# RWKV's triangular-inverse joins dealt among projections, and softmax's 1/sum put on a diagonal in the transposes

## Chip, cores and metric

The kernel runs on one core of one Trainium2 chip. The metric is the device time of one execution in microseconds (us), the median over runs. The engines are PE (matrix multiply; its weight loads are PEld), DVE (vector), ACT (scalar), POOL (GpSimd) and SP (which issues most DMAs). They work side by side, each through its own instructions in program order, and wait for one another by semaphores.

## What is computed

Two blocks of a language model over 1024 tokens of width 1024, in float32. The first is attention, cross attention and an MLP. The second block, in which the change lies, projects its input, mixes tokens in three ways at once and projects back:

```python
h = _rmsnorm(x, g_pre) * (1.0 + scale[:, None]) + shift[:, None]
proj = h @ w_in
...
attn = _sliding_window_attention(aq, ak, av, sinks)      # 8 heads, window 128, softmax with a sink
rwkv = _rwkv7_mixer(h, rr, rk, rv, ...)                  # 4 heads, a recurrence over tokens
gla = _gla_mixer(h, gq, gkk, gv, ...) * jax.nn.silu(gg)  # 4 heads, gated linear attention
y = jnp.concatenate([attn, rwkv, gla], axis=-1) @ w_out
return x + gate[:, None] * _rmsnorm(y, g_post)
```

The sliding attention's core is a softmax of which one column, the sink, is dropped again, and RWKV's recurrence is one step per token:

```python
p = jax.nn.softmax(jnp.concatenate([s, sink], axis=-1), axis=-1)[..., :-1]
o = jnp.einsum('bnhgqk,bnkhd->bnqhgd', p.astype(v.dtype), vb)
...
sa = jnp.einsum('bhvk,bhk->bhv', S, -kk_t)
S = (S * w_t[:, :, None, :] + sa[..., None] * (kk_t * a_t)[:, :, None, :]
     + v_t[..., None] * k_t[:, :, None, :])
```

## The kernel before, in words

Tokens go in two chunks of 512. For each chunk the second block has a stage for RWKV and GLA (`g_rec`, L1730) and one for the sliding attention (`g_window`, L1617; `g_window0` for chunk 0, `g_tail`, L1639, for chunk 1). `block2` (L1290) runs them in the order: chunk 0's `g_rec`, chunk 0's window, chunk 1's `g_rec`, chunk 1's window (called the tail below), then `finish`, which ends the output projection and the final norm of chunk 1.

PE has two sorts of work in these stages. The projections (`g_proj_F`, then the output projection `g_wout2`/`g_wout2a`) are long rows of 512-column matmuls at L210, L211 and L212: three per slice of 128 input rows, since each float32 product is made of high and low parts. They need nothing from the mixers. The mixers' own matmuls are small and hang on one another through DVE, ACT and POOL. `weave` (L144) deals the first out among the second: a mixer is a Python generator that yields a number after each piece; a positive number is the piece's own cost in ns and is multiplied by a ratio, a negative one is taken in full as a wait to be covered, and `weave` lets that many ns of projection slices (648 ns a slice) be issued there. The scheduler behind the language then moves single instructions within what the data allow, so the order on an engine is told by the built program. These projection matmuls are called fill below.

In `g_rec`, `early` (L1926) does RWKV. For 32 units (8 sub-chunks of 64 tokens by 4 heads) it inverts a triangular 64x64 matrix. First `s1` (L1780, L1786) makes the matrices with four groups of transposes and matmuls; `s2a` and `s2a_` (L1808, L1818) are PE work that hangs only on ACT. DVE alone solves the 16x16 diagonal blocks: four transposes (L1945), 15 steps of multiply and add (L1955, L1958), then two transposes that give TD (L1969) and more that fill U (L1978) and TQ. Then come the joins, which build the rest by matmuls on 32-row pieces:

- join 1, L1986: 64 matmuls with TD, which DVE turns into Y (L1988);
- join 2, L1994 and L1997: 96 matmuls with U and Y, copied out by ACT (L1998) and DVE (L2000);
- join 3, L2006: 32 matmuls, copied by ACT;
- join 4, L2013: 32 matmuls, copied by ACT.

A plain float32 matmul leaves two records in the trace, so the counts there are doubled. After the joins come `s2b` (L1828), `s2c` (L1842) and the recurrence `s3` (L1864 to L1881), with ACT and DVE steps between, and GLA's chain (`_gla`), whose main matmuls are L2156.

`w_units` (L1646) does the sliding attention, in 8 units per chunk (4 blocks of 128 queries by 2 groups of 4 heads). A unit's `a()` makes scores (L1668, L1669), adds the bias (DVE L1671), takes maxima (L1672), exponentials with their sums (ACT L1679), the reciprocal of the sum with the sink (DVE L1682, L1683), and then scales the probabilities `p` by it: two heads on ACT (L1685), two on POOL (L1686). `tr()` transposes each 128x128 piece of `p` on PE with the identity (L1700) and copies it out of PSUM (ACT L1703); `pv()` multiplies by the values (L1710), and DVE gates the result (L1712). A unit has 8 transposes, but 4 in each of the first two of chunk 0, so there are 120.

Beside the tail's output projection, `g_final0` (L2328) ends chunk 0's final norm. It is a generator as well, and `g_wout2a` (L2309) calls its next step after every second slice (after each in the first column block). Its first steps make a sum over partitions (L226), its inverse root (DVE L219, POOL L220) and two broadcasts by PE (L234), of `rf` and of `rz`; the others load, scale, add (DVE L2344, L2346, POOL L2347) and store one row block each.

Of the kernel before, what the change touches and what calls it, by code (L numbers as in the profile page):

```python
# [12 lines left out]
F32 = mybir.dt.float32  # L13
# [157 lines left out]
class K:  # L171
# [1118 lines left out]
    def block2(s, wp, pre, out):  # L1290
        tc, nc = s.tc, s.nc
        with tc.tile_pool(name="b2", bufs=1, reuse_waits="tile") as b2, tc.tile_pool(name="wk3", bufs=2, reuse_waits="tile") as s.wk, tc.tile_pool(
            name="smC", bufs=4, reuse_waits="tile"
        ) as s.sm:
            s.vt = b2.tile([P, NB, 400], F32, name="vt")
            s.b2_consts(b2)
            with tc.tile_pool(name="lo", bufs=1, reuse_waits="tile") as s.lop:
                with tc.tile_pool(name="wt", bufs=1, reuse_waits="tile") as wt:
                    with tc.tile_pool(name="pp", bufs=2, reuse_waits="tile") as pp:
                        vt = s.vt_load(wt, wp)  # L1300

                        def beside(m):
                            if m == 1:
                                hi = s.tl(s.xp, [P, KT, CH], "act", F32R)
                                lo = s.lop.tile([P, KT, CH], F32R, tag="lo1", name="lo1")
                                s.slow = s.fin_steps(1, hi, lo, s.wk)
                            for _ in range(2 if m >= 2 else 0):
                                next(vt, None)
                            if m == 7:
                                for _ in vt:  # L1310
                                    pass

                        for _ in chain(s.g_p2a(pp, 0, pre, beside), s.g_vt()):
                            pass
                rest = s.g_p2b(1)
                weave(
                    s.g_rec(0), chain(s.g_p2b(0), s.take(rest, s.K0)),
                    0.45
                )
                with tc.tile_pool(name="pp", bufs=2, reuse_waits="tile") as pp:  # L1320
                    weave(
                        s.g_window0(), chain(s.g_p2a(pp, 1), s.take(rest, s.K1)),
                        0.9
                    )
                    while s.steps:
                        s.steps.pop(0)()
                tp = ExitStack()

                def tail():
                    yield from s.g_tail(tp.enter_context(tc.tile_pool(name="tp", bufs=1, reuse_waits="tile")))  # L1330

                main = chain(s.g_rec(1), tail())
                rest = chain(rest, s.g_wout2(b2), s.g_wout2a(s.g_final0(b2, out)))
                weave(main, rest, 0.45, False)
                with tp, tc.tile_pool(name="fp", bufs=1, reuse_waits="tile") as fp:
                    s.finish(fp, wp, out, rest)

# [308 lines left out]
    def w_units(s, wn, c, qst, kst, bias, sink, one):  # L1646
# [6 lines left out]
        def unit(b, g):  # L1653
# [7 lines left out]
            def a():  # L1661
                p = u["p"] = wn.tile([P, 4, 2 * P], F32, tag="wp", name=s.nm("wp"), bufs=3)
                t = s.sm.tile([P, 6, 4], F32, tag="wt", name=s.nm("wt"))
                for z in range(2):
                    ps = s.ps([P, 2, 2 * P])
                    for y in range(2):
                        q = qst[2 * z + y][g][:, (b % 4) * P : (b % 4 + 1) * P]
                        mm(ps[:, y, :w], q, kst[g][:, k0 : k0 + w], start=True, stop=False)  # L1668
                        mm(ps[:, y, :w], q, kst[2 + g][:, k0 : k0 + w], start=False, stop=True)  # L1669
                    pz = p[:, 2 * z : 2 * z + 2, :w]  # L1670
                    V.scalar_tensor_tensor(pz, ps[:, :, :w], 0.125, bs[:, 2 * z : 2 * z + 2, :], ALU.mult, ALU.add)  # L1671
                    V.tensor_reduce(t[:, 0, 2 * z : 2 * z + 2], pz, AX.X, ALU.max)  # L1672
                sk = sink[:, 4 * g : 4 * g + 4]
                V.tensor_tensor(t[:, 1, :], t[:, 0, :], sk, ALU.max)
                V.tensor_tensor(t[:, 2, :], sk, t[:, 1, :], ALU.subtract)
                V.tensor_scalar(t[:, 1, :], t[:, 1, :], -1.0, None, ALU.mult)
                nc.scalar.activation(t[:, 2, :], t[:, 2, :], AF.Exp)
                for h in range(4):
                    nc.scalar.activation(  # L1679
                        p[:, h, :w], p[:, h, :w], AF.Exp, bias=t[:, 1, h : h + 1], accum_out=t[:, 3, h : h + 1]  # L1680
                    )
                V.tensor_tensor(t[:, 3, :], t[:, 3, :], t[:, 2, :], ALU.add)  # L1682
                V.reciprocal(t[:, 4, :], t[:, 3, :])  # L1683
                for h in range(2):
                    nc.scalar.activation(p[:, h, :w], p[:, h, :w], AF.Copy, scale=t[:, 4, h : h + 1])  # L1685
                nc.gpsimd.tensor_tensor(  # L1686
                    p[:, 2:4, :w], p[:, 2:4, :w], t[:, 4, 2:4, None].to_broadcast([P, 2, w]), ALU.mult
                )

            def tr():  # L1690
# [6 lines left out]
                for z in range(nk):  # L1697
                    ps = s.ps()
                    for h in range(4):
                        nc.tensor.transpose(ps[:, h * P : (h + 1) * P], u["p"][:, h, z * P : (z + 1) * P], s.ident)  # L1700
                    t = one[:, 4 + st["n"] % 4, :]
                    st["n"] += 1
                    nc.scalar.activation(t, ps, AF.Copy)  # L1703
# [41 lines left out]
    def rwkv(s, rp, ra, c):  # L1745
# [180 lines left out]
        def early():  # L1926
# [56 lines left out]
            for k in range(32):  # L1983
                for z in range(2):
                    a = slice(32 * z, 32 * z + 32)
                    mm(ps[a, k, :], XU[a, k, 1, a], TD[a, k, :], start=True, stop=True)  # L1986

            V.scalar_tensor_tensor(  # L1988
                Y, ps[0:64], s.m16[0:64, 0:1], s.m16[0:64, None, 1:17].to_broadcast([64, 32, 16]), ALU.mult, ALU.add
            )  # L1990
            yield -2000
            ps, pq = s.ps([P, 32, 16]), s.ps([P, 32, 16])
            for k in range(32):
                mm(pq[0:32, k, :], U[0:32, k, 0:32], Y[0:32, k, :], start=True, stop=True)  # L1994
                for z in range(2):
                    a = slice(32 * z, 32 * z + 32)
                    mm(ps[32 * z : 32 * z + 16, k, :], Y[a, k, :], U[a, k, 32 * z + 16 : 32 * z + 32], start=True, stop=True)  # L1997
            act(TQ[0:32, :, 0:16], pq[0:32], AF.Copy)  # L1998
            for z in range(2):
                V.tensor_copy(U[32 * z : 32 * z + 16, :, 32 * z + 16 : 32 * z + 32], ps[32 * z : 32 * z + 16])  # L2000
            yield 2000
            for g in range(2):
                ps = s.ps([P, 16, 32])
                for i in range(16):
                    k = 16 * g + i
                    mm(ps[32:64, i, :], XU[0:32, k, 1, 32:64], TQ[0:32, k, :], start=True, stop=True)  # L2006
                act(TQ[32:64, 16 * g : 16 * g + 16, :], ps[32:64], AF.Copy)
                yield 1000
            for g in range(2):
                ps = s.ps([P, 16, 32])  # L2010
                for i in range(16):
                    k = 16 * g + i
                    mm(ps[0:32, i, :], TQ[32:64, k, :], U[32:64, k, 32:64], start=True, stop=True)  # L2013
                act(U[0:32, 16 * g : 16 * g + 16, 32:64], ps[0:32], AF.Copy)
                yield (3860, 1000)[c]

            s2b(0)
            yield (1190, 1744)[c]
# [309 lines left out]
    def g_final0(s, b2, out):  # L2328
# [1 line left out]
        nc = s.nc  # L2330
        V = nc.vector
        r = s.sm.tile([P, 4], F32, tag="rz", name=s.nm("rz"))
        yield
        s.rsq(r, s.sums(s.zacc), 1.0 / D, EPS)
        RF = s.rst
        s.bcast(RF, s.rf[:, 0:4])
        yield
        RZ = s.zacc
        s.bcast(RZ, r)
        for mt in range(KT):  # L2340
# [113 lines left out]
```

## Time and profile before

| | |
|---|---|
| median of 3 runs | 2352.42 us (lowest 2352.35) |
| profiled execution: its time, its span from first to last instruction | 2354.5, 2352.7 us |
| busy share of the span: PE, DVE, ACT, POOL | 96%, 53%, 44%, 29% |
| mean granted PE clock, share of 2.4 GHz | 0.968 |
| second block's stages, from the first `s1` to the end | 1728.4 to 2352.7 us |

PE's busy time is modelled from starts, so a PE that is always busy can still be slow: its clock is granted at 2.4 or 1.2 GHz, and the share of it is given for each stretch as PEclk. A stretch of the trace is read by three things: how long PE waited and for whom, at which clock it ran, and what stood in its queue.

### The profile page before, as it was taken

To read this page: it belongs to the slowest core of one execution; us is meant where nothing else is said; L and a number is where in the kernel's file an instruction comes from. 1 tells how busy PE (TensorE), PEld (TensorE's weight loads), DVE (VectorE), ACT (ScalarE), POOL (GpSimd) and SP (SyncE) were. 2 spreads that over 40 slices of the span, in tenths; PEclk is the share of its full clock that TensorE was granted. 3 is DMA by queue.
4 is the path that set the end of the run, shared out by engine and by line. 5 is a ranking of instruction groups with operands and counts; after the bars stand their busy time and mean duration, and the time that the engine had idled before them with its cause. 6 is when DMAs were issued, how large, how long until landed. Compare 5 with 4: busy or idle time off the path is not lost. (4 is left out here: it accounts for less than half of the span.)

```text
span 2352.7 us, 36021 instructions
## 1 busy us (share of the span) xinstructions
PE 2255.0 (96%) x13696; PEld 1908.1 (81%) x13696; DVE 1251.6 (53%) x2266; ACT 1035.5 (44%) x2198; POOL 689.2 (29%) x1035
## 2 busy tenths in 40 slices
PE   8999999999999999999999999999999998999886
PEld 7898999988898888888888888888787875777765
DVE  7665656676754555423423322346842667526574
ACT  6655656674643424411311312344533357333563
POOL 4101100000500003566666630036321443214443
PEclk9999999999999999999999999999998999969997
DMA  4010010123241211222222211143342333424452
GB/s 135 28 41 23 30 39 28 46 78 122 68 137 54 99 36 50 77 74 79 83 74 79 79 59 51 48 134 121 116 128 76 113 121 118 147 74 134 154 173 75
DMA packets 116541, 200.14 MB, mean 85 GB/s; under 512 B 14192, under 2 KB 33936, under 8 KB 115600
## 3 DMA queue, kind: packets, MB, share of 16 engines
q1 hardware_dynamic: 111600, 184.73, 24.4%
q0 software_dynamic: 4768, 13.11, 1.7%
q8 instruction: 107, 1.75, 0.3%
q14 instruction: 66, 0.54, 0.1%
HBM read 163.71 MB, written 34.08 MB: 84 GB/s over the span
## 5 line engine op out<-in xcount | busy, mean ns | idle before, releaser
L210 PE MATMUL ps<-act,wh 128*128 128x512 f32 x1664 | 667.2, 404 | 8.8 <-ACT wh L202 5.4
L212 PE MATMUL ps<-act,wh 128*128 128x512 f32 x1664 | 658.5, 396 | 0.7 <-POOL wh L203 0.7
L211 PE MATMUL ps<-act,wh 128*128 128x512 f32 x1480 | 583.5, 394 | 3.5 <-DVE act L206 2.5
L202 ACT ACTIVATE wh<-stg 128x512 fp32r<-128x512 f32 x374 | 234.5, 629 | 579.6 <-PE ps L211 467.1
L210 PEld LDWEIGHTS ps<-act,wh 128*128 128x128 f32 x1664 | 317.5, 191 | 79.4 <-ACT wh L202 5.4
L212 PEld LDWEIGHTS ps<-act,wh 128*128 128x128 f32 x1664 | 317.0, 190 | 70.4 <-POOL wh L203 1.1
L211 PEld LDWEIGHTS ps<-act,wh 128*128 128x128 f32 x1480 | 281.6, 190 | 62.1 <-DVE act L206 3.5
L203 DVE TENSOR_TENSOR wh<-stg,wh 128x512 fp32r<-128x512 f32 x260 | 199.7, 770 | 156.4 <-ACT wh L202 154.4
L203 POOL TENSOR_TENSOR wh<-stg,wh 128x512 fp32r<-128x512 f32 x114 | 159.2, 1402 | 370.7 <-ACT wh L202 342.1
L909 DVE TENSOR_TENSOR act<-ps,act 128x512 f32<-128x512 f32 x112 | 77.0, 689 | 177.8 <-PE ps L212 177.7
L548 DVE TENSOR_TENSOR_SCAN pw<-pw,zero 128x128 f32<-128x128 f32 (+7 forms) x64 | 86.8, 1357 | 85.1 <-POOL pw L544 79.9
L249 POOL TENSOR_TENSOR nacc<-nacc,t 128x512 f32<-128x512 f32 x28 | 38.7, 1382 | 261.0 <-ACT t L248 256.6
L1146 DVE SCALAR_TENSOR_TENSOR t<-ps,Rm 128x512 f32<-128x512 f32 x64 | 44.1, 691 | 126.8 <-PE ps L212 126.1
L946 POOL TENSOR_TENSOR ad<-ad,cb 128x256 f32<-128x256 f32 x96 | 73.8, 769 | 125.7 <-DMA ad<-adaT 122.4
L951 POOL TENSOR_TENSOR ad<-ad 128x128 f32<-128x128 f32 (+5 forms) x288 | 97.7, 339 | 16.8
L210 PE MATMUL ps<-hid,wh 128*128 128x512 f32 x256 | 101.2, 395 | 0.0
L212 PE MATMUL ps<-hid,wh 128*128 128x512 f32 x256 | 101.1, 395 | 0.0
L211 PE MATMUL ps<-hid,wh 128*128 128x512 f32 x256 | 101.0, 394 | 0.0
L1147 ACT ACTIVATE t<-t 128x512 f32<-128x512 f32 x64 | 40.4, 632 | 135.8 <-DVE t L1146 135.8
L210 PE MATMUL ps<-wh,act 128*128 128x256 f32 x320 | 95.3, 298 | 0.0
L212 PE MATMUL ps<-wh,act 128*128 128x256 f32 x320 | 90.8, 284 | 0.0
L211 PE MATMUL ps<-wh,act 128*128 128x256 f32 x320 | 90.5, 283 | 0.0
(522 smaller groups left out, 4664.2 us busy)
## 6 DMA issues: line engine op xcount, KB each, us to landing
stg<-w2f SPq DMA_DIRECT2D x84, 256.0 KB, 2.8
stg<-w_dn SPq DMA_DIRECT2D x80, 256.0 KB, 2.7
stg<-w_up SPq DMA_DIRECT2D x64, 256.0 KB, 2.7
ad<-adaT POOLq DMA_DIRECT2D x96, 128.0 KB, 2.5
stg<-w2o SPq DMA_DIRECT2D x32, 256.0 KB, 2.7
pd<-t SPq DMA_DIRECT2D x30, 256.0 KB, 2.2
t<-yd SPq DMA_DIRECT2D x26, 256.0 KB, 3.5
rkd<-RK SPq DMA_DIRECT2D x4, 1280.0 KB, 5.2
```

What stands on the lines that cost most here:

```text
L202: nc.scalar.activation(hi, src, AF.Copy)
L203: (eng or nc.vector).tensor_tensor(lo, src, hi.bitcast(F32), ALU.subtract)
L210: mm(out, lh, rh, start=first, stop=False)
L211: mm(out, lh, rl, start=False, stop=False)
L212: mm(out, ll, rh, start=False, stop=last)
L249: nc.gpsimd.tensor_tensor(acc, acc, t[:, :n], ALU.add)
L548: V.tensor_tensor_scan(m[:, :w][:, ::-1], m[:, :w][:, ::-1], s.zero.to_broadcast([P, w]), 1.0, ALU.mult, ALU.add)
L909: s.nc.vector.tensor_tensor(hh, ps, hh, ALU.add)
L946: tt(t, t, cb[:, 256 * y : 256 * y + 256], ALU.mult)
L951: tt(acc[:, n, z, :] if w == 2 else a, a, b, ALU.add)
L1146: V.scalar_tensor_tensor(t, ps, 0.0, R[:, c * CH : (c + 1) * CH], ALU.max, ALU.mult)
L1147: nc.scalar.activation(t, t, AF.Square)
```

## The change

It has three parts. (1) The joins are dealt out: `early` now yields between parts of the joins, after every 8 units of join 1 (-1000 each) and of join 2 (-1400), and -700 or -1400 behind each join where there were 2000, 1000, 1000 and 3860 as costs. The ratios with which other costs are multiplied fall from 0.45 to 0.27 in chunk 0's `weave` and to 0.29 in the one of chunk 1 and the tail. (2) In the sliding attention `p` is no longer scaled. POOL writes the four heads' reciprocals on four diagonal 128x128 matrices (identity times a broadcast column, a new tile `wd` with 3 buffers), and the transposes become plain float32 matmuls of `p` with its diagonal, which transpose and scale in one. (3) `g_final0` yields once more ahead of its sums and three times more between its two broadcasts, so that its later steps come that many calls later.

```diff
-                    0.45
+                    0.27
...
-                weave(main, rest, 0.45, False)
+                weave(main, rest, 0.29, False)
...
                 V.reciprocal(t[:, 4, :], t[:, 3, :])
-                for h in range(2):
-                    nc.scalar.activation(p[:, h, :w], p[:, h, :w], AF.Copy, scale=t[:, 4, h : h + 1])
+
+                dg = u["d"] = wn.tile([P, 4, P], F32, tag="wd", name=s.nm("wd"), bufs=3)
                 nc.gpsimd.tensor_tensor(
-                    p[:, 2:4, :w], p[:, 2:4, :w], t[:, 4, 2:4, None].to_broadcast([P, 2, w]), ALU.mult
+                    dg, s.ident[:, None, :].to_broadcast([P, 4, P]), t[:, 4, :, None].to_broadcast([P, 4, P]), ALU.mult
                 )
...
                     for h in range(4):
-                        nc.tensor.transpose(ps[:, h * P : (h + 1) * P], u["p"][:, h, z * P : (z + 1) * P], s.ident)
+                        mm(
+                            ps[:, h * P : (h + 1) * P], u["p"][:, h, z * P : (z + 1) * P], u["d"][:, h, :],
+                            start=True, stop=True,
+                        )
...
                     mm(ps[a, k, :], XU[a, k, 1, a], TD[a, k, :], start=True, stop=True)
+                if k % 8 == 7:
+                    yield -1000
...
-            yield -2000
+            yield -700
             ps, pq = s.ps([P, 32, 16]), s.ps([P, 32, 16])
             for k in range(32):
...
+                if k % 8 == 7:
+                    yield -1400
             act(TQ[0:32, :, 0:16], pq[0:32], AF.Copy)
...
-            yield 2000
+            yield -700
+
...
-                yield 1000
+                yield -1400
...
-                yield (3860, 1000)[c]
+                yield -1400
...
-        yield
+        for _ in range(2):
+            yield
         s.rsq(r, s.sums(s.zacc), 1.0 / D, EPS)
         RF = s.rst
         s.bcast(RF, s.rf[:, 0:4])
-        yield
+        for _ in range(4):
+            yield
```

On PE in chunk 1, from the end of join 2 to `s2b`, there stood before (L2006 and L2013 are joins 3 and 4, L1828 is `s2b`, L212 is fill):

```order
L1997 MATMUL ps_19411<-act_18928,t_3437_19306 16x16 x2
L212 MATMUL ps_19407<-act_15525,wh_19271 128x512
L2006 MATMUL ps_19515<-act_18928,XT 32x32 x16
L2006 MATMUL ps_19536<-act_18928,XT 32x32 x16
L2013 MATMUL ps_19557<-act_18928 32x32 x16
L2013 MATMUL ps_19575<-act_18928 32x32 x16
L1828 MATMUL ps_19596<-AV_19206,act_18928 64x128 x4
```

and now the same joins (L2014, L2021; `s2b` is L1831) stand so, with the last two of 21 fill rows ahead of them:

```order
L211 MATMUL ps_19523<-lo_15526,wh_19394 128x512
L212 MATMUL ps_19523<-act_15525,wh_19395 128x512
L2014 MATMUL ps_19563<-act_18920,XT 32x32 x16
L2014 MATMUL ps_19587<-act_18920,XT 32x32 x16
L2021 MATMUL ps_19611<-act_18920 32x32 x16
L210 MATMUL ps_19652<-act_15525,wh_19513 128x512
L211 MATMUL ps_19652<-lo_15526,wh_19513 128x512
L212 MATMUL ps_19652<-act_15525,wh_19514 128x512
```

Nine fill rows in all stand between the halves of join 4 and six behind it, where there were none. From the first row of join 1 to the first row of `s3`, fill rows go from 36 to 84 in chunk 0 and from 30 to 87 in chunk 1; from `s1` to join 1 they fall from 90 to 72 and from 81 to 66; from `s3` to L2205 from 198 to 165 and from 220 to 186. Over the whole of a chunk's `g_rec`, up to L2255, there are as many as before: 378 and 369.

On ACT in chunk 0's window, around the scaling of the sixth and seventh unit (L1679 exponentials, L1527, L1530 and L1586 other functions, L202 a weight's high half, L1703 the copy of transposed pieces), there stood before:

```order
L1679 ACTIVATE wp_18713,wt_18714<-wp_18713,wt_18714 128x256 x4
L1527 ACT_TABLE_LOAD
L1527 ACTIVATE pt_18684<-pt_18684 128x512
L202 ACTIVATE wh_18852<-stg_18850 128x512
L1586 ACT_TABLE_LOAD
L1586 ACTIVATE t_3352_18840<-ps_18758 128x512
L1685 ACTIVATE wp_18622<-wp_18622,wt_18623 128x256 x2
L1685 ACTIVATE wp_18713<-wp_18713,wt_18714 128x256 x2
```

The two L1685 rows are gone, and nothing of the scaling stands behind the table loads any more. On PE the pieces of that sixth unit, two of its transposes at first, stood ahead of the next unit's scores (L1668):

```order
L1700 MATMUL ps_18795<-ident,wp_18622 128x128
L1700 MATMUL ps_18801<-ident,wp_18622 128x128
L1668 MATMUL ps_18813<-k_3186_17963,act_17966 128x256
L1669 MATMUL ps_18813<-k_3188_17965,act_17966 128x256
L1668 MATMUL ps_18813<-k_3186_17963,act_17966 128x256
```

and now all eight do, with the diagonal `wd` in the identity's place:

```order
L212 MATMUL ps_18751<-act_15525,wh_18560 128x512
L1700 MATMUL ps_18788<-wd_18643,wp_18617 128x128 x4
L1700 MATMUL ps_18794<-wd_18643,wp_18617 128x128 x4
L1668 MATMUL ps_18806<-k_3186_17963,act_17966 128x256
L1669 MATMUL ps_18806<-k_3188_17965,act_17966 128x256
```

The six transposes that came later, after ten rows of fill, have moved up to the other two; as many fill rows (24) stand ahead of the unit as before, between it and the unit two ahead.

## Rows read from the trace of the kernel before

**Rows 1.** Busy time by stage: stretch, length, PE, PEld, DVE, ACT, POOL, PEclk, DMA.

```profile
1728.40:1898.40 170.00, 162.44 (x1644) 130.42 (x1642) 86.94 (x194) 60.22 (x115) 49.79 (x41) 0.92 0.30 96
1898.40:2010.20 111.80, 100.03 (x461) 74.80 (x462) 79.77 (x161) 75.16 (x174) 44.74 (x35) 0.95 0.44 143
2010.20:2204.20 194.00, 178.75 (x1658) 142.61 (x1657) 100.47 (x217) 75.58 (x147) 53.69 (x43) 0.86 0.34 108
2204.20:2308.40 104.20, 90.14 (x436) 69.79 (x437) 70.47 (x117) 60.74 (x156) 48.40 (x36) 0.92 0.55 180
```

**Rows 2.** Six stretches in which the clock was low, same columns.

```profile
1764.50:1778.50 14.00, 10.34 (x239) 9.28 (x234) 6.25 (x8) 0.68 (x2) 0.00 (x0) 0.51 0.08 30
1983.00:1993.50 10.50, 3.73 (x14) 3.44 (x15) 5.79 (x12) 8.47 (x18) 4.23 (x3) 0.51 0.16 51
2037.50:2041.50 4.00, 4.00 (x13) 3.18 (x12) 3.69 (x14) 2.64 (x5) 0.58 (x1) 0.57 0.16 54
2047.50:2051.50 4.00, 4.00 (x50) 3.29 (x45) 3.09 (x4) 0.00 (x0) 0.00 (x0) 0.57 0.48 134
2058.00:2089.00 31.00, 28.78 (x299) 24.34 (x296) 5.01 (x12) 7.63 (x13) 1.26 (x1) 0.50 0.21 66
2245.50:2253.00 7.50, 4.26 (x15) 3.74 (x15) 5.82 (x13) 4.68 (x15) 3.61 (x4) 0.54 0.10 37
```

**Rows 3.** PE in order of time around the joins: start, length, what, count.

```profile
1776.48 0.63 PE L212 MATMUL ps<-act,wh 128*128 128x512 f32 x1
1776.91 0.63 PE L210 MATMUL ps<-act,wh 128*128 128x512 f32 x1
...
1779.18 0.39 PE L211 MATMUL ps<-act,wh 128*128 128x512 f32 x1
1779.40 0.39 PE L212 MATMUL ps<-act,wh 128*128 128x512 f32 x1
...
1780.86 2.21 PE L2006 MATMUL ps<-act,XT 32*32 32x32 f32 x64
...
2045.96 2.24 PE L1986 MATMUL ps<-t,XT 32*32 32x16 f32 x128
...
2062.25 3.46 PE L2006 MATMUL ps<-act,XT 32*32 32x32 f32 x61
```

**Rows 4.** PE's waits from 1724 us on: waited in total, times, longest.

```profile
PE ps L1700 <- ACT wp L1685: 14.5, 3, 8.6
PE ps L2156 <- ACT t L248: 6.6, 1, 6.6
PE ps L234 <- POOL rz L220: 5.4, 2, 4.3
PE ps L1710 <- ACT act L1703: 4.4, 4, 3.4
PE ps L1994 <- DVE t L1988: 3.7, 1, 3.7
...
PE ps L1828 <- ACT AV L1819: 2.1, 3, 0.7
PE ps L1842 <- ACT WT L1832: 1.7, 1, 1.7
```

**Rows 5.** DVE in order of time: TD's two transposes, chunks 0 and 1.

```profile
1760.69 2.15 DVE L1969 STREAM_TRANSPOSE t<-act 32x512 f32<-32x512 f32 x2
...
2042.18 2.32 DVE L1969 STREAM_TRANSPOSE t<-act 32x512 f32<-32x512 f32 x2
```

**Rows 6.** PE: eight plain float32 matmuls, and a unit's eight transposes.

```profile
2218.71 1.95 PE L2266 MATMUL ps<-ident,go 128*128 128x128 f32 x16
...
2255.41 1.04 PE L1700 MATMUL ps<-ident,wp 128*128 128x128 f32 x8
```

**Rows 7.** PE and DVE in order of time at the longest wait in chunk 0's window.

```profile
1989.77 0.69 PE L1700 MATMUL ps<-ident,wp 128*128 128x128 f32 x2 [8.58 <-ACT wp L1685]
...
1983.62 0.17 DVE L1683 RECIPROCAL wt<-wt 128x4 f32<-128x4 f32 x1
```

**Rows 8.** POOL by line and form: count, busy, mean ns.

```profile
L1686 POOL TENSOR_TENSOR wp<-wp,wt 128x512 f32<-128x512 f32 x14 | 16.1, 1149 | 27.9 <-DVE wt L1683 9.0 <-ACT wh L202 7.6 <-ACT act L1703 6.8
...
L2124 POOL TENSOR_TENSOR act<-ident,gd 128x512 f32<-128x512 f32 x4 | 5.5, 1388 | 0.2 <-ACT gd L2121 0.2
```

## The prediction

> **What bounds the kernel now.** I read the busy time by stage first [rows 1]. In each of the four stages PE is busy for 86 to 96% of the time and DVE, the next engine, for 71% at most, so PE sets the pace. The fill can be moved anywhere, and the order counts as many fill rows after the change as before (378 and 369 in the two `g_rec`). So only two sorts of loss can be won back: time in which PE waits, and time in which it runs at half clock. The low clock is the larger one: PEclk is 0.86 in chunk 1's `g_rec`, the lowest of the stages. The second view is those low stretches alone [rows 2]. The longest, 2058 to 2089, has 28.78 us of busy PE in 31.00 us at 0.50, that is 1.2 GHz, and it begins in the joins. The third view is PE in order of time [rows 3]: neighbouring fill rows start 0.43 us apart in the low stretch of chunk 0 (1776.48, 1776.91) and 0.22 to 0.23 apart behind it (1779.18, 1779.40). I use 0.228 as the price of a fill at full clock, and 0.20 as its loss at half. Join 3 took 2.21 us for 64 records in chunk 0 and 3.46 for 61 in chunk 1: 1.64 times as much per record, not 2. The fourth view is PE's waits [rows 4]: 14.5 us for the scaling on ACT (L1685) in three waits, 6.6 for L248, 5.4 for `rz` on POOL, 4.4 for the copies L1703, 3.7 and 2.2 inside the joins.
>
> All terms below are us against the profiled execution (2354.5, span 2352.7); minus is faster. That execution stands 2.1 above the median of 2352.42, and the difference is carried to the median.
>
> **Joins of chunk 0.** The dealt fill comes partly from ahead of join 1, where rows fall from 90 to 72. DVE finishes TD at 1760.69 + 2.15 = 1762.84 [rows 5], and PE already waited 0.7 for it [rows 4], so all cover taken away opens as a wait: 17 rows (with one for slack in the order) by 0.228 = +3.9. The 3.7 us wait for Y (L1988) now has fill of its own: -3.7. Of the low stretch 1764.5 to 1778.5 [rows 2], nine fill rows lose 0.20 each and now stand elsewhere: -1.8. The joins themselves stay slow there, for the new wait in front of them is just what lets the clock fall; 12 of the rows dealt among them cost 0.20 more each: +2.4. From `s3` on there are 33 fewer rows as cover, and the waits at L1828 and L1842 can come again. They are 2.1 and 1.7 long in all [rows 4]; the bounds are 0 and 3.8, and I take +2.0, near the middle. Sum: 3.9 - 3.7 - 1.8 + 2.4 + 2.0 = **+2.8**.
>
> **Joins of chunk 1.** TD is there at 2042.18 + 2.32 = 2044.50 [rows 5], and join 1 began at 2045.96 [rows 3], 1.46 later. Fifteen rows fewer in front are 3.42 less, so a wait of 1.96 opens; with the low stretch at 2037.5 [rows 2] gone as well (1.7 of its 4.00) it is 3.66. I take the middle, +2.8. The two short low stretches have 4.00 us each at 0.57; at full clock each would take about 2.3: -1.7 twice. The dealt rows: 15 of them at half clock, +3.0. The wide stretch from 2058 is the main term. Here the trace of before doesn't show the clock for joins with this much fill in them. The nearest rows on both sides: chunk 1's joins, with a single fill between join 2 and join 3, stayed at 1.2 GHz; chunk 0's joins 3 and 4, with three or four rows between, ran at 2.4 GHz behind the fill that ended at 1779.4 [rows 3]. The order now puts 21 rows ahead of join 3, nine between the halves of join 4 and six behind it, which is nearer to chunk 0. So the low stretch's busy time, 28.1 of the 28.78 that belong to joins and `s2b`, comes down by 1 - 1/1.64: -11.0. If the clock stays low all the same, this term is 0. The fill is missing later: over some 4 us `s2c` and `s3` now alternate with no fill between. Waits there, as in chunk 0, +2.0, and one more short low stretch, +1.7. The 6.6 us wait of L2156 for L248 [rows 4] finds other PE work ahead of it in the new order, since rows L2205 to L2255 stand differently; its bounds are -6.6 and 0, and I take -2.0, nearer to nothing, since ACT's queue in front of L248 is unchanged. Sum: 2.8 - 3.4 + 3.0 - 11.0 + 2.0 + 1.7 - 2.0 = **-6.9**.
>
> **The transposes.** Eight transposes take 1.04 us, and eight plain float32 matmuls of that shape (L2266, 16 records) 1.95 [rows 6]: +0.91 for eight, 0.114 each. Over all 120 that is +13.7: 56 in chunk 0's window, 6.4, and 64 in the tail, 7.3. ACT loses 32 scalings. POOL's scaling took 1149 ns, and a diagonal of the same size, L2124, 1388 [rows 8]; POOL has room, 40 to 46% busy in these stages [rows 1].
>
> A rule of the Trainium skill speaks against this part more loudly: "TensorE: Matmul & The Clock Gate", section "Terms", says that the transpose mode of trn2 is four times faster for float32. By it a plain matmul would cost 0.39 more than a transpose, and 120 of them 46.8. The rows show 1.9 times, not four, and I go by the rows.
>
> **Chunk 0's window.** Its longest wait is the 8.58 us before 1989.77 for ACT's scaling [rows 7], though the reciprocal was finished at 1983.62 + 0.17 = 1983.79: ACT was held by exponentials, table loads and a weight half ahead of the scaling in its queue. Now the transposes hang on POOL's diagonal: 1983.79 + 1.39 and a hand-over make 1985.5. PE would have waited from 1981.19, and the 32 dearer transposes before this place bring it there 3.65 later, inside the wait. So the wait ends 4.3 earlier: -4.3, with those 32 paid in it. The other 24 come behind it: +2.7. The low stretch at 1983.0 has 3.73 of busy PE at half clock [rows 2]; a full cure gives 1.9, and I take -1.5 as the rest of the wait still comes. Sum: **-3.1**.
>
> **Tail.** The transposes: +7.3. `g_final0` asks for the `rz` broadcast four calls later, with 6 fill rows, matmuls of L1710, transposes and scores ahead of it, so the 4.3 us wait [rows 4] goes: -4.3. The low stretch at 2245.5, which follows this wait, has 4.26 of busy PE at half clock [rows 2]; half its excess over full clock and a little more goes: -1.7. The other waits there are the two of L1700 besides the long one (14.5 - 8.6 = 5.9) and the 3.4 of L1710 [rows 4], 9.3 in all. They go with ACT's scaling or take dearer transposes in; between 0 and 9.3 I take half, -4.6. Sum: **-3.3**. The final norm's loads, multiplications and stores of chunk 0 also come four calls later on SP, POOL and DVE. I cost that at nothing: the end hangs on chunk 1's projection, and DMA is at 0.55 of its time in the stage [rows 1]. If the stores slid behind the tail's last fill, it would be a microsecond or two.
>
> **Sum.** 2.8 - 6.9 - 3.1 - 3.3 = -10.5. The profiled execution would come to 2344.0, and the median to 2352.4 - 10.5 = **2341.9**.
>
> **Rivals.**
>
> (A) The clock holds everywhere and no new wait opens. For it: the joins are the place where the clock fell, and a PE fed with fill keeps it in chunk 0 [rows 3]. Against: TD is late in both chunks [rows 5]. Then my added terms go: 3.9 + 2.4 + 2.0 in chunk 0 and 2.8 + 3.0 + 2.0 + 1.7 in chunk 1, 17.8 in all: 2324.1.
>
> (B) The matmuls cost their full price and no wait takes it in. The place is the stretch between POOL's diagonal and PE's transposes: POOL also makes weight halves, and if one of these stands ahead of the diagonal, then PE waits for POOL as long as it did for ACT. This decides once the diagonal ends later than the old scaling did, 1989.77 in the long wait. Window: +6.4 in place of -3.1. Tail: 7.3 - 4.3 - 1.7 = +1.3 in place of -3.3. That is 14.1 dearer than my sum: -10.5 + 14.1 = +3.6, 2356.0. For it: 13.7 us of surely added PE work. Against: POOL's idle share.
>
> (C) The change does not do what it says: the clock won in the joins is paid back in waits before join 1 and in `s3`, to a net of nothing, 2352.4. For it: as many fill rows as before, merely moved.
>
> (D) The transposes' price is far from the one of L2266. At 0.39 each in place of 0.114, as four times the measured 1.04 for eight makes it, 33.1 are added to my sum: 2375.0. Against it stand the measured L2266 rows, whose shape is the same [rows 6].
>
> **How the numbers follow.** The forecast has 0.43, A 0.22, B 0.22, C 0.10, D 0.03. The forecast's own range is 2334 to 2351: the main term may be 7 to 13, and the waits may move by 4 each way. The full range is 2323 to 2360: down to A, up past B with some microseconds for the stores. Outside lie D, the half of A that is faster still, and little else, some 0.17. Two per cent is 47 us, about what a measurement of this kernel can surely tell from no change. Faster than 2305 would need more than the whole of A, 0.02; slower than 2399 needs D and more, 0.01; within is 0.97.
>
> **What would show it right or wrong.** In the changed profile, chunk 1's `g_rec` should have a PEclk near 0.92 and join 3 should take about 2.2 us; if it takes 3.4 again the main term has failed. In the view of waits there should be no ACT L1685, a wait before join 1 of 4 to 5 us in chunk 0 and 2 to 4 in chunk 1, and no 4.3 us for `rz`. Eight transposes should take 1.95; 1.04 would give back 13.7, over 3 would speak for D. The wait of window 0 should end near 1985.5 on its own scale, for POOL; if the page names POOL with over 6 us there, B was right. Waits of more than 4 us in `s3`, or a PEclk there under 0.8, would make C right.

## The result, and the profile after

The changed kernel takes 2367.22 us (median of 7 runs, 2364.55 to 2371.99); its time stands to that of the kernel before as 1.0055, 95% interval 1.0041 to 1.0068. That is some 13 us slower, where the forecast was 10.5 faster, and 2367.22 lies outside the stated range of 2323 to 2360. (Of the seven runs of the kernel before beside it, one took 4421.85 us and is left out; the others took 2351.78 to 2360.63.) The profiled execution is one of 2364.68 us with a span of 2362.9.

The busy time by stage of the kernel after, with the columns of [rows 1]: RWKV's `s1`, joins, `s3`, the end of GLA and the window of chunk 0, then the same for chunk 1 and the tail (to PE's last matmul):

```profile
1725.63:1758.30 32.67, 29.98 (x199) 22.87 (x197) 24.89 (x60) 15.03 (x28) 8.55 (x7) 0.95 0.37 122
1758.30:1805.86 47.56, 46.76 (x597) 36.52 (x597) 11.03 (x15) 12.69 (x20) 8.94 (x7) 0.79 0.22 68
1805.86:1889.61 83.75, 80.84 (x767) 64.68 (x766) 47.71 (x110) 29.93 (x62) 28.88 (x23) 0.93 0.29 96
1889.61:1938.91 49.30, 43.48 (x209) 33.94 (x207) 19.65 (x36) 20.37 (x34) 18.65 (x16) 0.88 0.37 123
1938.91:2022.77 83.86, 78.75 (x395) 60.22 (x393) 63.78 (x135) 52.38 (x130) 30.10 (x23) 1.00 0.43 134
2022.77:2055.17 32.40, 30.10 (x193) 22.30 (x192) 25.90 (x65) 15.90 (x29) 6.84 (x6) 0.95 0.36 113
2055.17:2097.56 42.39, 42.16 (x599) 33.04 (x599) 13.27 (x20) 13.66 (x24) 8.93 (x7) 0.92 0.35 114
2097.56:2201.90 104.34, 87.17 (x787) 70.54 (x787) 60.43 (x125) 43.38 (x87) 33.38 (x27) 0.87 0.35 109
2201.90:2233.37 31.47, 31.47 (x171) 25.43 (x170) 9.54 (x16) 11.78 (x21) 15.10 (x10) 0.95 0.43 142
2233.37:2350.72 117.35, 105.56 (x625) 88.12 (x623) 82.97 (x145) 58.38 (x157) 49.69 (x43) 0.95 0.42 137
```

The table reads them against the same stretches of before. Fill moved between stages, so a length alone says nothing: the fill rows that came or went are taken off at 0.228 us each. What is left over is what the change cost there. The predicted column regroups the terms of the sum by stage.

| stage | length before, after | fill rows | left over | predicted |
|---|---|---|---|---|
| chunk 0: `s1` to join 1 | 33.56, 32.67 | -18 | +3.2 | +3.9 |
| join 1 to `s3` | 33.67, 47.56 | +48 | +3.0 | -3.1 |
| `s3` to L2205 | 87.67, 83.75 | -33 | +3.6 | +2.0 |
| L2205 to the first scores | 41.44, 49.30 | +3 | **+7.2** | 0 |
| window | 85.44, 83.86 | 0 | -1.6 | -3.1 |
| chunk 1: `s1` to join 1 | 35.76, 32.40 | -15 | +0.1 | +1.1 |
| join 1 to `s3` | 37.34, 42.39 | +57 | -7.9 | -9.7 |
| `s3` to L2205 | 104.52, 104.34 | -34 | **+7.6** | +1.7 |
| L2205 to the first scores | 32.59, 31.47 | -5 | 0.0 | 0 |
| tail | 120.16, 117.35 | -3 | -2.1 | -3.3 |

The last column sums to -10.5, the one before it to +13.1. (The spans of the two profiles differ by only 10.2, because chunk 0's `s1` begins 2.8 us earlier in the second, ahead of all that was changed.) The clock in chunk 1's joins went as forecast: PEclk there is 0.92 in place of 0.62. In this profile two stages that the prediction hardly looked at took more than the gain back. The first row below is one of PE's waits of the kernel before, the others are those of the kernel after (its L2164 is L2156 of before, L2258 and L2263 are L2250 and L2255, L1713 is L1710, L1989 is L1986):

```profile
PE ps L2255 <- ACT go L2250: 0.8, 1, 0.8
```
```profile
PE ps L2164 <- DVE act L2176: 14.2, 4, 12.0
PE ps L1700 <- POOL wd L1686: 6.5, 3, 3.7
PE ps L2263 <- ACT go L2258: 5.8, 1, 5.8
PE ps L1713 <- ACT act L1706: 5.3, 4, 2.7
...
PE ps L1989 <- DVE t L1972: 2.2, 4, 1.0
```

Against [rows 4], L1685 and the long `rz` wait are gone and so are the two waits of join 2 (L1994). In their place stand 12.0 us in one wait of GLA's matmuls L2164 and 5.8 in one of L2263; the latter was 0.8 before. The clock is low in and behind both (columns as above; the first stretch is the one around chunk 0's dealt joins):

```profile
1754.50:1775.50 21.00, 19.23 (x164) 13.96 (x162) 11.02 (x21) 3.73 (x5) 2.55 (x2) 0.51 0.07 27
1915.00:1925.50 10.50, 7.40 (x23) 6.24 (x24) 3.43 (x5) 4.56 (x8) 1.27 (x1) 0.51 0.16 50
2184.50:2205.50 21.00, 9.03 (x64) 7.75 (x61) 10.30 (x20) 9.74 (x18) 0.00 (x0) 0.51 0.28 80
```

**The wait of chunk 0.** ACT in order of time at the end of its `g_rec`, first two rows of the kernel before, then the kernel after, and PE at the wait:

```profile
1898.93 0.62 ACT L457 ACTIVATE k<-ws 64x512 fp32r<-64x512 f32 x1
...
1906.61 1.15 ACT L2250 ACTIVATE go<-act 128x512 f32<-128x512 f32 x2
```
```profile
1907.26 0.63 ACT L202 ACTIVATE wh<-stg 128x512 fp32r<-128x512 f32 x1 [1.26 <-PE ps L211]
1907.91 0.59 ACT L1452 ACTIVATE t<-ps 64x512 f32<-64x512 f32 x1
1908.53 0.64 ACT L457 ACTIVATE k<-ws 64x512 fp32r<-64x512 f32 x1
...
1913.00 2.57 ACT L443 ACTIVATE act<-ws 64x512 fp32r<-64x512 f32 x4
1915.60 0.63 ACT L1459 ACTIVATE lora<-lora 64x512 f32<-64x512 f32 x1
1916.13 1.26 ACT L443 ACTIVATE act<-ws 64x512 fp32r<-64x512 f32 x2
1917.42 1.15 ACT L2258 ACTIVATE go<-act 128x512 f32<-128x512 f32 x2
```
```profile
1918.10 1.87 PE L2263 MATMUL ps<-b,go 128*128 128x2 f32 x8 [5.82 <-ACT go L2258]
```

L2263 needs two squares on ACT (L2258). Ahead of them in ACT's queue stand the splits of the window's keys and queries (L457, L458, L443), which need no PE work. Ahead of those now stand a weight half, L202, which waited for the fill at L211, and a copy, L1452. The splits began 3.1 us after the last L2242 (1905.40), where they had begun 0.5 after the same copy in the kernel before (L2234, 1898.43). Two more L443 and L1459 also came ahead of the squares, which so began 12.0 us after that copy in place of 8.2. The clock is 0.51 up to 1925.5, behind the wait.

**The wait of chunk 1.** DVE, ACT and PE at the wait, then SP's queue, in order of time (`yf` is RWKV's output, `bd` and `pd` its two inputs read back, `ws` the window's keys and queries):

```profile
2182.18 0.68 DVE L1926 TENSOR_TENSOR yf<-yf,t 128x512 f32<-128x512 f32 x1
2182.78 1.42 DVE L2176 COPY_PREDICATED act<-gm,ps 128x256 f32<-128x256 int32 x4
2186.55 0.28 DVE L459 TENSOR_TENSOR k<-ws,k 64x128 fp32r<-64x128 f32 x1 [2.35 <-ACT k L457]
...
2192.33 5.71 DVE L444 TENSOR_TENSOR act<-ws,act 64x512 fp32r<-64x512 f32 x8 [0.62 <-ACT act L443]
2198.07 2.93 DVE L2176 COPY_PREDICATED act<-gm,ps 128x256 f32<-128x256 int32 x8
```
```profile
2186.21 0.31 ACT L457 ACTIVATE k<-ws 64x128 fp32r<-64x128 f32 x1 [5.74 <-DMA ws<-pd]
```
```profile
2198.56 1.96 PE L2164 MATMUL ps<-gX 32*128 32x64 f32 x8 [11.97 <-DVE act L2176]
```
```profile
2169.15 0.42 SPq L1394 DMA_DIRECT2D t<-bd  x1
2169.62 0.42 SPq L1394 DMA_DIRECT2D t<-pd  x1
2170.14 0.38 SPq L1391 DMA_DIRECT2D zd<-t  x1
...
2175.91 0.33 SPq L1391 DMA_DIRECT2D yd<-yf  x1
2176.29 0.42 SPq L1394 DMA_DIRECT2D t<-bd  x1
...
2182.89 0.32 SPq L1391 DMA_DIRECT2D yd<-yf  x1
2183.63 0.33 SPq L1596 DMA_DIRECT2D sink<-sink  x1
2184.02 0.60 SPq L1602 DMA_DIRECT2D ws<-pd  x1
```

PE waits for the mask copies L2176. DVE has them behind the splits L459 and L444, these wait for the reads of `ws`, and SP issues these reads behind RWKV's second store `yd`. This store waits for its loads, which SP issued behind the first store: both pairs of loads go into tiles `t2`, whose five buffers they share with the results of the projections. Before, both pairs were issued before the first store:

```profile
2163.01 1.36 SPq L1394 DMA_DIRECT2D t<-bd  x1
...
2168.05 3.81 SPq L1391 DMA_DIRECT2D yd<-yf  x2
...
2174.18 0.42 SPq L1602 DMA_DIRECT2D ws<-pd  x1
```

The chain was there before (8.7 us in two waits); now it has one more round in it. What this round costs is less sure than that it is there: the other five kernels below whose chunk 1 is dealt and that keep the old loads have it too, and their waits of these matmuls sum to 8.4 to 10.9 us in that stage, where the changed kernel has 13.7.

### The profile page after: what moved, and what is told of

Same layout as the page of the kernel before. It is cut to its first block, busy times and chain, and to the rows that moved or that the text cites. A ratio compares the mean times of both kernels' runs of the same rounds, so it can differ in the third digit from the quotient of the medians.

```text
span 2362.9 us, 36219 instructions
## 1 busy us (share of the span) xinstructions
PE 2268.4 (96%) x13816; PEld 1917.3 (81%) x13816; DVE 1254.7 (53%) x2266; ACT 1025.1 (43%) x2166; POOL 689.5 (29%) x1035
## 5 line engine op out<-in xcount | busy, mean ns | idle before, releaser
L212 PE MATMUL ps<-act,wh 128*128 128x512 f32 x1664 | 661.7, 398 | 0.8 <-POOL wh L203 0.8
L211 PE MATMUL ps<-act,wh 128*128 128x512 f32 x1480 | 586.6, 397 | 2.4 <-DVE act L206 1.3
L202 ACT ACTIVATE wh<-stg 128x512 fp32r<-128x512 f32 x374 | 234.6, 629 | 595.0 <-PE ps L211 487.9
L212 PEld LDWEIGHTS ps<-act,wh 128*128 128x128 f32 x1664 | 319.2, 192 | 71.0 <-POOL wh L203 1.2
L211 PEld LDWEIGHTS ps<-act,wh 128*128 128x128 f32 x1480 | 283.5, 192 | 59.7 <-DVE act L206 1.8
L212 PE MATMUL ps<-hid,wh 128*128 128x512 f32 x256 | 101.1, 395 | 0.0
L211 PE MATMUL ps<-hid,wh 128*128 128x512 f32 x256 | 101.0, 394 | 0.0
L212 PE MATMUL ps<-wh,act 128*128 128x256 f32 x320 | 90.7, 284 | 0.0
L211 PE MATMUL ps<-wh,act 128*128 128x256 f32 x320 | 90.4, 282 | 0.0
```

Source lines behind the costliest of these rows:

```text
L202: nc.scalar.activation(hi, src, AF.Copy)
L211: mm(out, lh, rl, start=False, stop=False)
L212: mm(out, ll, rh, start=False, stop=last)
```

## The experiments

Phase lengths of one profile vary by some us where the clock decides (last section), so verdicts go by the ratios, to the kernel before, with 95% intervals. Sixteen more kernels were timed; all lie within 1.2% of the kernel before.

**Each part alone.** Parts as numbered in the section on the change; the other parts are as before.

> The kernel before with part 1 alone: joins dealt in both chunks, ratios 0.27 and 0.29. Theory (T): the loss is made by dealing chunk 0's joins; between the two profiles chunk 0's g_rec grew by 16.9 us, from s1 to the window's first scores, while chunk 1's hardly moved (+0.4). So this kernel is about 15 us slower than before, ratio 1.0065, and shows the low clock from before join 1 of chunk 0 on and the wait of L2255 for ACT. Rival (R): the joins are neutral and the price of the 120 plain matmuls, 13.7 us, is the loss: ratio 1.000.

Measured: 1.0082 (1.0065 to 1.0099), 19 us slower.

> The kernel before with part 2 alone: diagonals on POOL, plain matmuls for the transposes. T: the matmuls stand in waits that were there, the window and the tail come out even or up to 4 us faster (in the changed profile they were 1.6 and, with part 3, 2.8 shorter): ratio 0.998 to 1.000. R: the price is paid in full, +13.7 us: ratio 1.006.

Measured: 0.9989 (0.9976 to 1.0002).

> The kernel before with part 3 alone: chunk 0's final norm four calls later. T: the 4.3 us wait for rz goes, with the low clock behind it, 2 to 6 us faster: ratio 0.998. R says the same or, if other waits in the tail take its place, 1.000.

Measured: 0.9987 (0.9974 to 0.9999). The three add up to 1.0058, the changed kernel's 1.0055: the joins alone make the loss, and part 2, price and gain together, moves the time by nothing that its interval shows. Rival B falls for the window (83.89 us with part 2 alone, 85.44 before).

**Chunk 0's joins undealt.**

```diff
-                    0.27
+                    0.45
-                if k % 8 == 7:
+                if c == 1 and k % 8 == 7:
...
-                yield -1400
+                yield (3860, -1400)[c]
```

> The changed kernel, but chunk 0 with the old yields and the old ratio 0.45; chunk 1's joins stay dealt, parts 2 and 3 stay. T: chunk 0's 16.9 us come back, about 17 faster than the changed kernel and some 4 faster than before: ratio 0.998 to before. R: no gain over the changed kernel, ratio 1.005.

Measured: 0.9973 (0.9961 to 0.9985). About 19 us come back, so the loss is made by dealing chunk 0.

> The kernel before with parts 2 and 3, no join dealt. If the parts add: 0.9989 of part 2 and 0.9987 of part 3 give 0.9976 to before, as the kernel in which chunk 1 alone is dealt (0.9973). Then dealing chunk 1's joins is worth nothing. If chunk 1's joins are a gain of their own, this kernel is 3 to 7 us slower than that one: 0.999 to 1.000.

Measured: 0.9981 (0.9970 to 0.9991). Dealing chunk 1's joins moves the time by nothing that these intervals show, though PEclk from its join 1 to `s3` is 0.81 in the profile with them dealt and 0.62 without.

**Two repairs of the changed kernel**, one for each wait. The first also issues the load of the window's bias behind the squares, which now stand in its room.

```diff
+            g = s.g_gla_out(mx, 0)
+            x = next(g)
             for _ in s.win_load(mx, 0):
...
+        es = new() if c else s.go[:, 0:2, :]
```

> The changed kernel, but the squares that L2255's matmuls read (ACT, L2250 before) are issued ahead of the window's splits of queries and keys, and into room that they don't share with them. Theory: in chunk 0 the 5.8 us wait of L2255 is ACT's queue, in which these splits stand first, and the low clock of 1915 to 1925 follows from that wait; both go, L2205 to the first scores shrinks from 49.3 to some 42 us, about 7 faster than the changed kernel, ratio 1.003 to before. Rival: the 33 fill rows that were dealt away are missing here, and another wait of 4 to 6 us takes the place of this one: ratio 1.0055 as the changed kernel.

Measured: 1.0003 (0.9989 to 1.0018), 12 faster than the changed kernel, where 7 was expected. No wait of L2255's matmuls is left, and L2205 to the first scores takes 40.7 us. That holds in every profile: 48.1 to 49.3 us in the five kernels with chunk 0 dealt and the squares in their old place, 39.0 to 40.7 in the three with the repair. The rest of this profile doesn't fit the theory: from `s3` to L2205 chunk 0 takes 6 us more, at a clock of 0.85, and chunk 1 takes 9 less (95.1), though its loads are as they were. The wait of L2164 (here L2175) is 8.7 in it, and 8.4 in the coarser deal further down, again with the old loads (first and second row):

```profile
PE ps L2175 <- DVE act L2187: 10.1, 2, 8.7
```
```profile
PE ps L2164 <- DVE act L2176: 9.8, 2, 8.4
```

So what the other 5 of the 12 us are made of stays open.

```diff
-            bo, sg = s.tl(s.wk, [P, CH], "t2"), s.tl(s.wk, [P, CH], "t2")
+            xf = XT.rearrange("p a b c d e -> p (a b c d e)")
+            bo, sg = xf[:, 1024 * pr : 1024 * pr + 512], xf[:, 1024 * pr + 512 : 1024 * pr + 1024]
```

> The changed kernel, but RWKV's output step (two loads, scale, gate, store, for each of two row blocks) loads into room of its own and not into the tiles t2 that it shares with the projections' results. Theory: in chunk 1 the second pair of loads stood behind the first store on SP, with it the window's reads, and so DVE's splits of them ahead of the mask copies of L2168; with early loads the 12 us wait of L2156 falls to 6 or less, the low stretch behind it from 20.5 to under 10, s3 to L2205 of chunk 1 from 104.3 to 95 to 99 us, ratio 1.002 to before. Rival: the cover of 34 fill rows is missing there, and waits of the same sum stay whatever SP does: 104, ratio 1.0055.

Measured: 1.0029 (1.0015 to 1.0042), 6 faster than the changed kernel. SP's queue and PE's wait in its trace (L2165 is L2156 of before):

```profile
2177.70 0.93 SPq L1391 DMA_DIRECT2D yd<-yf  x2
2179.02 0.33 SPq L1596 DMA_DIRECT2D sink<-sink  x1
2179.42 0.43 SPq L1602 DMA_DIRECT2D ws<-pd  x1
```
```profile
PE ps L2165 <- DVE act L2177: 7.1, 3, 5.3
```

Both stores go out together, the reads follow at once, and the wait falls from 12.0 to 5.3. The stage itself, 99.8 us, missed its 95 to 99, and the low stretch behind the wait, 13.7 us, its 10. Chunk 0's `s3` to L2205 gained 3 as well (80.7), for the same loads stand there. In chunk 1 the repair shows in the waits rather than in the length: with its joins dealt the waits sum to 6.5 to 7.5 us in the five kernels with it and 8.4 to 13.7 in the six without, while the stage takes 92.5 to 99.8 us with it and 92.7 to 105.3 without. How much of chunk 1's +7.6 the order on SP made is therefore not shown; of the 6 us by which the time fell, some 3 stand in chunk 0.

> The changed kernel with both repairs. If they add (1.0003 and 1.0029 in place of 1.0055): 0.998. Then what is left of chunk 0's dealing against the kernel with chunk 1 alone dealt and the repairs (0.995) is the low clock among its dealt joins and the cover taken from ahead of join 1, some 6 us. Rival: the two repairs cure the same wait, 1.000 or more.

Measured: 0.9956 (0.9940 to 0.9971), better than the sum of the two. Chunk 0 from L2205 to the first scores, then chunk 1 from `s3` to L2205:

```profile
1891.73:1930.77 39.04, 39.04 (x208) 30.55 (x207) 23.77 (x38) 20.49 (x34) 21.71 (x18) 1.00 0.47 155
2087.80:2180.27 92.47, 82.83 (x788) 67.06 (x787) 60.46 (x124) 43.46 (x87) 32.50 (x27) 0.92 0.38 123
```

No idle time and no low clock is left in the first, where the changed kernel had 5.8 and 0.88.

**The same repairs with less dealing.**

> Parts 2 and 3 with both repairs and no join dealt. Theory: the waits that the repairs cure are smaller without dealing (0.8 for L2255, 8.7 in two waits for L2156, which stands behind the same reads), so they gain 1 to 4 us over parts 2 and 3 alone: 0.996 to 0.997. If it equals the kernel with chunk 1 dealt and the repairs, dealing is worth nothing even with its waits cured.

Measured: 0.9967 (0.9954 to 0.9980).

> The kernel with chunk 1 alone dealt and parts 2 and 3, and with both repairs: the squares ahead of the splits, RWKV's output loads in room of their own. Theory: the repair on SP takes 5 to 6 us of chunk 1's wait away (ratio 0.9973 becomes 0.995), the squares add nothing since chunk 0 isn't dealt and its wait was 0.8. Rival: the wait returns elsewhere, 0.997.

Measured: 0.9971 (0.9960 to 0.9983); the 0.995 was missed. The repairs are worth 0.0099 with all joins dealt (1.0055 to 0.9956) and 0.0014 with none (0.9981 to 0.9967). The difference, 0.0085 or 20 us, is as large as the loss of part 1 alone. So with the two repairs dealing comes to nothing that the times show: it had lost by what it made the queues do. In the profiles that nothing is a sum. With all joins dealt and both repairs chunk 0 is still 8.8 us longer up to its first scores than with none dealt (201.4 and 192.6), and chunk 1 with the tail 8.3 shorter.

**How finely the joins are dealt.** `k % 4 == 3` with -500 and -700 in joins 1 and 2, and `k % 16 == 15` with -2000 and -2800.

> The changed kernel with joins 1 and 2 dealt twice as finely: after every 4 units, half the amount each. As much fill as in the changed kernel, but up to 8 more places in each chunk where PE goes from joins to fill and back. Theory: such a place costs 0.2 to 0.3 us (the last fill of a run stood 0.21 longer than its pitch), so join 1 to s3 grows by some 2 us in each chunk, 47.6 to 49.5 and 42.4 to 44.5: ratio 1.007. Rival: the loss of chunk 0's joins is the clock alone; a finer mixture holds it as well or better, join 1 to s3 stays or shrinks: ratio 1.0055 or less.

Measured: 1.0114 (1.0094 to 1.0134); join 1 to `s3` took 59.3 and 45.0 us. Chunk 1 grew by 2.6, near the 2 expected. Chunk 0 grew by 11.7, for the clock stayed low through `s2b` and `s2c`:

```profile
1797.50:1822.00 24.50, 24.50 (x149) 18.98 (x147) 2.36 (x8) 3.58 (x6) 1.26 (x1) 0.51 0.28 85
```

> The changed kernel with joins 1 and 2 dealt half as finely: after every 16 units, twice the amount each, as much fill. Theory: each place where PE goes to fill and back costs 0.2 to 0.3 us, and the finer deal cost 11.7 and 2.6 us from join 1 to s3 by keeping the low clock beside; the coarser one has some 4 places fewer, so join 1 to s3 takes 45 to 47 in chunk 0 (47.6 in the changed kernel) and 40 to 42 in chunk 1 (42.4): ratio 1.003 to 1.005 to before. Rival: places cost nothing, the clock alone decides, and it falls with long runs of small matmuls: 47.6 or more in chunk 0, 42.4 or more in chunk 1, ratio 1.0055 or more.

Measured: 1.0022 (1.0007 to 1.0037); 46.3 us in chunk 0, as expected, but 43.4 in chunk 1, where 40 to 42 was expected. The time falls with coarser dealing in both steps (1.0114, 1.0055, 1.0022), in the last one by more than the 1.003 expected at best. But in this profile the largest gain over the changed kernel, 11.7 us, is in chunk 1 from `s3` to L2205 (92.7), which the edit doesn't touch. The profiles don't separate the price of a place from the clock that goes with it either, so that stays open.

**Part 2 in chunk 0's window alone**, the tail scaling as before (`if c == 1:` the old lines).

> The kernel before with part 2 in chunk 0's window alone (the tail scales as before) and part 3; no join is dealt. If the parts add up by stages: the window 83.9 in place of 85.4, the tail 113.8 in place of 120.2 as with part 3 alone, the rest as before: 8 faster, ratio 0.9965. Rival: the tail's gain of part 3 alone was partly chance of one profile; then 3 to 5 faster, ratio 0.998.

Measured: 0.9978 (0.9967 to 0.9989): the rival's figure. The tail took 115.1 us, not 113.8.

> Chunk 1 alone dealt, both repairs, part 3, and part 2 in chunk 0's window alone; the tail scales as before. Theory: chunk 0's g_rec as undealt (191 to 193 us from s1 to the first scores), chunk 1 as dealt and repaired (198 to 202), and the tail without the price of 64 plain matmuls, 2 to 3 shorter than the 118 it took with them (115.1 with part 3 and old scaling): 2344, ratio 0.9955. Rival: the tail's waits take the matmuls in, so it stays at 118: 0.997 as with the diagonals in both.

Measured: 0.9955 (0.9936 to 0.9975). The tail took 111.6 us; with the diagonals and the same joins it took 117.9. One profile each is a weak witness here, and with no join dealt the same two tails differ by 1.3 (115.5 and 116.9). The times agree better: with chunk 1, both chunks or none dealt, the kernels with the old scaling in the tail are 0.0016, 0.0016 and 0.0014 faster (this and the next two runs against those with both repairs), about 3.5 us, though the intervals of each pair overlap. So part 2 seems to cost the tail about half of the 7.3 us of its plain matmuls.

> Joins dealt in both chunks as in the changed kernel, both repairs, part 3, diagonals in chunk 0's window alone. If stages add: the kernel with all parts and both repairs (0.9956) less the tail's matmuls, some 3 us: 0.9943. Rival, by the stages of the profiles: dealing chunk 0 still costs some 9 us after the repairs, so it is slower than the kernel with chunk 1 alone dealt (0.9955): 0.998 to 0.999.

Measured: 0.9940 (0.9921 to 0.9959), 2340.28 us, the lowest ratio of all: 0.6% faster than the kernel before and 1.1% faster than the changed one. The rival fell.

> No join dealt, both repairs, part 3, diagonals in chunk 0's window alone. If dealing is worth nothing once its waits are cured, this equals the kernel with chunk 1 alone dealt (0.9955) and the one with both (within 0.0015). If chunk 1's joins are a gain of 5 to 7 us with the reads cured, this is slower by that: 0.998.

Measured: 0.9953 (0.9936 to 0.9971). With one, both or no chunk dealt the repaired kernels take 0.9955, 0.9940 and 0.9953: the intervals overlap, and a gain of dealing isn't shown.

## Why the prediction was wrong, point by point

- **The step that failed** is the one that priced the stretches from which fill was taken. Between -10.5 and +13.1 lie 23.6 us: 7.2 of them in chunk 0 from L2205 on, 6.1 in its joins, 5.9 in chunk 1 from `s3` on. For chunk 0 "the waits at L1828 and L1842 can come again", +2.0, was all from `s3` on, and from L2205 on there was no term. The runs show +3.6 and +7.2 there: the first fell by 3 with the loads in room of their own, the second came by a wait that grew from 0.8 us to 5.8 and by the low clock behind it. At 0.8 it was too small to stand among the rows that I chose. That chunk 0 makes the loss is shown by the kernel with its joins undealt (0.9973), and this wait by the repair. I looked for the waits that would go and for the cover of those that I saw. I did not ask which transfers and ACT steps a shifted fill would put into a new order.
- **L2156 and chunk 1.** "I take -2.0, nearer to nothing, since ACT's queue in front of L248 is unchanged": it was +5 (8.7 us of waits became 13.7 in the stage). The name L248 misled me. It was the releaser that came last, but DVE's L2168 stood behind the same reads of the window, and SP's order in front of those had changed. How much of the +7.6 of this stage that order made stays open: in the six kernels with it the stage takes 92.7 to 105.3 us, at clocks of 0.93 to 0.81.
- **Chunk 1's clock, right in kind.** -9.7 was forecast from join 1 to `s3`, and -7.9 measured; in the other eight profiles with the same deal it is -10.3 to -2.2. Some of the nearness is luck, since a reading behind the -11.0 was wrong: of the 28.78 us busy in the low stretch 15.2 belong to joins and `s2b`, not 28.1; 4 are `s2c`, 6 are fill and the rest is mostly the beginning of `s3`. By the same rate 15.2 would have given -5.9. Over the 194 us of [rows 1] from chunk 1's `s1` on PEclk came to 0.89, from 0.86, and not to the 0.92 that was named. Join 3 ran at full clock in the changed kernel (55 records in 1.92 us):

```profile
2079.26 1.92 PE L2014 MATMUL ps<-act,XT 32*32 32x32 f32 x55
```

- **Chunk 0's joins, wrong in sign.** The wait for Y went as said (-3.7), but the low clock around the joins grew from 14 to 21 us, and each run of fill between them stood some 0.2 us longer than its rows at their pitch, in 12 runs up to `s3` (at full clock the first and the last row of one took 0.33 and 0.32 us to the next start, in place of 0.23).
- **Wait before join 1, right in sum.** +3.9 forecast, +3.2 measured. As a wait for TD it was 2.2 us in both chunks together (0.7 before); the rest was low clock ahead of it and a longer wait for ACT at L1821. So the named sign, 4 to 5 us of wait, was not seen.
- **The plain matmuls' price, right.** 1.95 us for eight, as L2266 [rows 6]:

```profile
2314.59 1.95 PE L1700 MATMUL ps<-wd,wp 128*128 128x128 f32 x16
```

  The factor four of the Trainium skill ("TensorE: Matmul & The Clock Gate", "Terms") is not seen here; it is 1.9. Rival D is out.
- **Window, right in kind:** -1.6 for -3.1. The same unit's wait of 8.58 us for ACT became one of 1.27 for POOL. It ended at 1999.64; since the window begins 14.15 later in this profile, that is 1985.49 on the scale of before, and 1985.5 was named:

```profile
1999.64 2.05 PE L1700 MATMUL ps<-wd,wp 128*128 128x128 f32 x16 [1.27 <-POOL wd L1686]
```

- **Tail, right in sum, partly by luck:** -2.1 for -3.3. Part 2 alone was to gain there, its 7.3 less 4.6 of waits and the cured low clock; by the times above it cost about 3.5. The gain was that of the later `rz`: with part 3 alone the tail took 113.8 us, 6.4 less than before.
- **Rivals.** A needs that the added waits don't come, and they came: it falls. B holds for about half of the tail's price, not for the window. C came nearest in kind (the clock's gain is paid back in waits, one of them over 4 us in the stage from `s3` on, as its sign says), but it ended at nothing.

## What to carry to other kernels

Fill that is moved keeps its sum but changes which weight halves, stores and loads stand ahead of what in ACT's, DVE's and SP's queues. So before such a change is priced, read the order of those queues around the places that lose fill, small waits included. Where a deal of work loses, look for shared buffers and for steps queued behind work that isn't needed yet: with two such places mended, the same deal was 23 us faster. A gain of the clock in one stage is worth only what the next stages leave of it: chunk 1's joins alone dealt ran at 0.81 in place of 0.62, and the time moved by nothing that shows (0.9973 and 0.9981).

## What the runs showed that was not expected

By the profile's count PE was busy without a gap and yet stayed at the low clock: 24.50 of 24.50 us at 0.51 in the finer deal, with fill between the small matmuls. In the changed kernel the same stage, from join 4 to `s3`, ran at full clock.

Which of the two comes isn't set by the order within the stage alone. Chunk 1's stretch from join 1 to `s3`, with 87 rows of fill and the joins dealt alike, took 40.1 to 48.2 us in the profiles of nine kernels, at clocks of 0.98 to 0.79. In five of them the runs of fill stand between the joins in the very same lengths, and they took 42.3 to 48.2. What ahead of the stage decides it is not shown. One profile is no verdict on such a stage.
